# A hybrid decoder layer on one core: the recurrence's rounds joined in pairs, the first gate sums moved to another engine

## The chip, the cores and the metric

The kernel runs on one core of a Trainium2 chip. Five engines work side by side, each with its own queue of instructions: TensorE (PE in the profile; its weight loads are PEld), VectorE (DVE), ScalarE (ACT), GpSimd (POOL) and SyncE (SP, which here only issues DMAs). They wait for each other by semaphores. Matmul results go to PSUM, which is allotted here in banks of 128 partitions by 512 four-byte columns; everything else lies in SBUF. The metric is the device time of one execution in microseconds; the times below are the median of 3 runs.

## The reference, cut to what matters

One layer on x of 1024 tokens by 1024 channels (batch 1): a joint projection, three branches (an RWKV-7 recurrence with 8 heads of 64, a stick-breaking attention, a cross-attention to 256 memory tokens), gates, an output projection, and a convolutional feed-forward part. The change touches the first norm, the recurrence and the feed-forward part:

```python
h = rms_norm(x, norm1_g);  proj = h @ w_in
# recurrence, one token t, per head; S is 64x64
sa = einsum('bhij,bhj->bhi', S, -kk_t)
S  = S * w_t + sa[..., None] * (kk_t * a_t) + v_t[..., None] * k_t
y_t = einsum('bhij,bhj->bhi', S, r_t)
...
h   = rms_norm(x, norm2_g) @ w_up               # 1024 -> 2 * 2816
acc = conv_b + causal_conv_width_3(h, conv_w)
gate, val = split(acc, 2);  x = x + (silu(gate) * val) @ w_down
```

## The kernel before

All large products are float32 products made of three: every operand is split into a high part, which ACT copies (L81, L1502), and a low part, the rest, which POOL or the DVE subtracts (L82, L1505); high by high, high by low and low by high are added in PSUM. Every matmul is issued by one helper (L123), every transposing one by another (L106), so the profile tells matmuls apart by their tiles: `mm` and `g` are the PSUM banks of the large products (128x512) and of the rest.

**Startup.** The projection of the first columns runs over eight blocks of x (`units`, `part_units`), while ACT squares the blocks and the DVE adds the squares (L221). `row_norm` sums the squares over the channels with 32 tiny matmuls and turns them into a factor per token, `row_spread` spreads it. `row_norm` stands inside the fifth block of the second group of columns.

**The recurrence (`stage2`).** The 1024 tokens are 16 chunks of 64, two to a group of 128; the 8 heads are 4 pairs `p`. Within a chunk the recurrence is rewritten as products of 64x64 matrices with the running state `U`. Each pair has a PSUM bank of its own in a chunk (tag `g`, four of them), with 64 columns each for A, Y, W and S. A chunk has three rounds:

1. state products into A and products with `M` onto it, and the DVE copies A into `ys` (L638);
2. products into W, which ACT copies (L649);
3. state products into Y; then, pair by pair, products onto Y, products into S, the DVE's update of the state from S (L659), and ACT's two copies of Y into the output (L661).

Between two rounds `weave` runs steps of the other work (the gates' and the output projection's large products, called filler here), 2.15 steps a round on average, in practice 12 or 18 large matmuls. Every third round or so a part of the output's norm (L680 to L694) is given out, too. The DVE and ACT take their work in the order in which a scheduler put it; among it are evacuations of the filler's banks (L1263).

**The feed-forward part (`up_phase`).** The two-by-two product of weights and tokens is done in seven products instead of eight, on sums of blocks. A loop runs over pairs `n` of weight tiles; `step(n, i)` issues product `i` and what follows from it on the DVE; `prep1`, `prep2`, `prep3` and `second_sums` make the sums and the parts of later weights, mostly on POOL (L1505 low parts, L1520 and L1521, L1540 and L1541 sums). For n=2 the order is 5, 6, 2, 7, 4, 3. Each finished pair of tiles is convolved (`conv`: ACT L1574, DVE L1575, L1584) and becomes a gated tile in `g_all` (L1580, L1587, L1592). `act_sums` makes four sums of the gated tile's quarters for the down phase (DVE, L1600) and stores sums and quarters from ACT's queue (L1605, L1609, L1610). For the first tile it is called in step 6 and step 7 of n=2, where L1637 adds step 6's result, and L1646 and L1647 add step 7's; TensorE's step 3 takes the bank that L1647 reads. L1659 and L1668 follow steps 4 and 3.

Of the kernel before, what the change touches and what calls it, by code (L numbers as in the profile page):

```python
# [49 lines left out]
class Trunk:  # L50
# [135 lines left out]
    def startup(self):  # L186
# [104 lines left out]
        nc.sync.dma_start(self.lora, self.I["lora"])  # L291
        self.seg = self.t4("A")
        nc.sync.dma_start(self.seg, self.I["seg"])
        units(1, [4])
        part_units(1, 5, ((0, 0),), None)
        self.row_norm(sqs[-1])
        part_units(1, 5, ((1, 0), (0, 1)), None)
        units(1, [6, 7])
        units(2, [4])
        self.row_spread()  # L300
# [276 lines left out]
    def stage2(self):  # L577
        nc = self.nc
        self.y = [self.t4("qk") for _ in range(4)]
        vs = self.t4("ys", n=512)  # L580
        it = self.t4("it")
        ut = it[:, 0:512].rearrange("p (u c) -> p u c", u=8)
        U = [[ut[:, 2 * p + i] for i in range(2)] for p in range(4)]
        self.ordered(nc.gpsimd.memset(ut, 0.0))
        hq = [slice(0, 64), slice(64, 128)]
        heads = [(p, h2) for p in range(4) for h2 in range(2)]
        A, Y, W, S = (slice(o, o + 64) for o in range(0, 256, 64))
        Ms = self.t4("at")
        Ls, VTs = {}, {}
        norm = iter(())  # L590

        def load_l(g):
            for p in range(3):
                L = self.t4("at")
                nc.sync.dma_start(L, self.scr[p, g])
                Ls[g, p] = L[:, 0:256], L[:, 256:512], L[:, 512:1024]
            M = Ms[:, g % 2 * 512 : g % 2 * 512 + 512]
            nc.sync.dma_start(M, self.scr[3, g][:, 512:1024])
            Ls[g, 3] = [None, None, M]

        def load_v(g):
            for k in range(2):
                V2 = self.t4("qk")
                for h2 in range(2):
                    nc.sync.dma_start(V2[hq[h2], h2 * 256 : h2 * 256 + 256], self.vd[k, h2, g].rearrange("s c i -> s (c i)"))
                nc.sync.dma_start(V2[:, 512:768], self.td[k, g].rearrange("h s p i -> (h s) (p i)"))
                for i in range(2):
                    VTs[g, 2 * k + i] = [V2[:, h2 * 256 + i * 128 : h2 * 256 + i * 128 + 128] for h2 in range(2)], V2[:, 512 + i * 128 : 640 + i * 128]
                nc.sync.dma_start(V2[:, 768:1024], self.scr[3, g][:, k * 256 : k * 256 + 256])
                Ls[g, 3][k] = V2[:, 768:1024]  # L610

        load_l(0)
        yield
        load_v(0)
        for _ in range(2):
            yield
        for c in range(NC):
            g, cc = c // 2, c % 2
            us = []
            for p in range(4):  # L620
                (RA, BT, MT), (V, TT) = Ls[g, p], VTs[g, p]
                us.append((
                    U[p][cc], U[p][1 - cc], RA[:, cc * 128 : (cc + 1) * 128], BT[:, cc * 128 : (cc + 1) * 128],
                    MT[:, cc * 256 : (cc + 1) * 256], [v[:, cc * 64 : (cc + 1) * 64] for v in V],
                    TT[:, cc * 64 : (cc + 1) * 64], vs[:, p * 64 : (p + 1) * 64], self.ps("g")))

            def state(o, rs):
                for p, h2 in heads if c else ():
                    Uo, _, ra, _, _, _, _, _, pb = us[p]
                    q = hq[h2]  # L630
                    self.mmul(pb[q, o], ra[q, rs], Uo[q], start=True, stop=False)

            state(A, Y)
            for p, h2 in heads:
                _, _, _, _, M, wv, _, v1, pb = us[p]
                self.mmul(pb[hq[h2], A], M[hq[h2], h2 * 128 + 64 : h2 * 128 + 128], wv[h2][hq[h2]], start=(c == 0), stop=True)
                if h2 == 1:
                    nc.vector.tensor_copy(v1, pb[:, A])  # L638
            yield
            next(norm, None)  # L640
            if not cc and g + 1 < NG:
                load_l(g + 1)
                load_v(g + 1)
            for p, h2 in heads:
                _, _, _, _, _, wv, tt, v1, pb = us[p]
                self.mmul(pb[hq[1 - h2], W], tt[hq[h2]], v1[hq[h2]], start=True, stop=True)
                if h2 == 1:
                    for q, w in zip(hq, wv[::-1]):
                        nc.scalar.activation(w[q], pb[q, W], AF.Copy)  # L649
            yield  # L650
            next(norm, None)
            state(Y, A)
            for p, (Uo, Un, ra, bt, M, wv, tt, v1, pb) in enumerate(us):
                for h2, q in enumerate(hq):
                    self.mmul(pb[q, Y], M[:, h2 * 128 : h2 * 128 + 64], wv[h2], start=(c == 0), stop=True)
                if c < NC - 1:
                    for h2, q in enumerate(hq):
                        self.mmul(pb[q, S], bt[:, q], wv[h2], start=True, stop=True)
                    nc.vector.scalar_tensor_tensor(Un, Uo, self.pc[p][:, c : c + 1], pb[:, S], ALU.mult, ALU.add)  # L659
                for h2, q in enumerate(hq):  # L660
                    nc.scalar.activation(self.y[p][cc * 64 : cc * 64 + 64, g * 128 + h2 * 64 : g * 128 + h2 * 64 + 64], pb[q, Y], AF.Copy)  # L661
            yield
            next(norm, None)
            if c % 4 == 3:
                for _ in norm:
                    pass
                norm = self.norm_quarter(c // 4, it[:, 512:1024])
        for _ in norm:
            pass
        for _ in range(4):  # L670
            yield
# [803 lines left out]
    def up_phase(self, raws, t2, operand, split_hi, split_lo, sums, norm, spread):  # L1475
# [21 lines left out]
                    if n < 3:  # L1497
                        self.pinned(ins)

        def hl(src, pool, tags, n=1024, keep=False, queue=False, eng=nc.gpsimd):  # L1500
            hi, lo = (pool.tile([128, n], F32R, name=self.nm(t), tag=t, bufs=16 if t == "l4" else 2) for t in tags)
            ins = nc.scalar.activation(hi, src, AF.Copy)  # L1502
            if keep:
                self.pinned(ins)
            ins = eng.tensor_tensor(lo, src, hi.bitcast(F32), ALU.subtract)  # L1505
            if queue:
                self.tc.keep_in_program_order(ins)
            return hi, lo

        L, R = slice(0, 512), slice(512, 1024)  # L1510
# [21 lines left out]
        def prep3(n):  # L1532
            if n == 0:
                w2, s4 = self.early[2], self.early[3][:, R]
            else:
                w1, w2 = W.pop(n)
                s = st.pop((n, "s"))
                s4 = self.pool_r.tile([128, 512], F32, name=self.nm("s4"), tag="s4", bufs=1)
                fix = self.tc.keep_in_program_order if n == 1 else lambda ins: ins
                fix(nc.gpsimd.tensor_tensor(w2[:, L], w1[:, L], w2[:, L], ALU.subtract))  # L1540
                fix(nc.gpsimd.tensor_tensor(s4, w1[:, R], s[:, R], ALU.subtract))  # L1541
            w = hl(w2, self.pool_wt, ("wh", "wl"), keep=n < 2, queue=n < 2, eng=nc.gpsimd if n else nc.vector)
            st[n, 7], st[n, 4] = [[x[:, c] for x in w] for c in (L, R)]
            if n == 1:
                return s4
            if n:
                st[n, 3] = hl(s4, self.pool_l, ("l4", "l4"), 512)
# [50 lines left out]
        def act_sums(f, late):  # L1598
            a11, a21, a12, a22 = (g_all[:, j] for j in range(4))
            tt = lambda o, x, y, op: self.pinned(nc.vector.tensor_tensor(o, x, y, op))  # L1600
            if not late:
                tt(sa[:, 0], a21, a22, ALU.add)
                tt(sa[:, 1], sa[:, 0], a11, ALU.subtract)
                for j, src in ((0, a11), (1, a12), (3, a22)):
                    nc.scalar.dma_start(self.actd[f, j], src)  # L1605
            else:
                tt(sa[:, 2], a11, a21, ALU.subtract)
                tt(sa[:, 3], a12, sa[:, 1], ALU.subtract)
                nc.scalar.dma_start(self.actd[f, 2], sa[:, 3])  # L1609
                nc.scalar.dma_start(self.actd[f, 4:7].rearrange("i p t -> p i t"), sa[:, 0:3])  # L1610

        def evacuate(n):
            p1 = st[n, "p1"] = self.r4("p1", n=512)
# [4 lines left out]
        def step(n, i):  # L1618
# [13 lines left out]
            elif i == 6:  # L1632
# [4 lines left out]
                self.pinned(nc.vector.tensor_tensor(st[n, "u1"][:, R2], Bk, st[n, "p1"], ALU.add))  # L1637
                if n == 2:
                    st.pop((1, "gates"))[1]()
                if n and pairs[n - 1][2]:  # L1640
                    act_sums(pairs[n - 1][1], n > 2)
            elif i == 7:
                Bk = st.pop((n, "B"))
                product(n, 7, Bk, False, True)
# [2 lines left out]
                ins = nc.vector.tensor_tensor(v[:, R2], st[n, "C"], v[:, L2], ALU.add)  # L1647
                if n == 2:
                    self.pinned(ins)
                    act_sums(pairs[n - 1][1], True)  # L1650
            elif i == 40:
                Dk = st[n, "D"] = bank()
                product(n, 4, Dk, True, True)
# [93 lines left out]
        for n in range(1, len(pairs)):  # L1747
# [3 lines left out]
            for i in order:  # L1751
# [17 lines left out]
                if n > 1 and i == 2:  # L1769
                    prep1(nxt)  # L1770
                    if n == 2:
                        second_sums(4)
                if i == 3:
                    prep3(nxt)

# [173 lines left out]
    def run(self):  # L1949
# [74 lines left out]
        st2 = self.stage2()  # L2024
        next(st2)
        need("y1")
        self.weave(st2, pump, 2.15, 0)
        self.weave(self.group_norm(), pump, 1, 0)
        drain(pump)
        self.close_gates()  # L2030
# [81 lines left out]
```

## Time and profile before

| | |
|---|---|
| median of 3 runs | 1774.13 us (1772.08 to 1774.95) |
| the profiled execution | 1774.39 us, its span 1772.6 us |
| TensorE busy | 1762.3 us, 99% |
| weight loads (beside it) | 1442.4 us, 81% |
| DVE, ACT, POOL busy | 1180.0, 864.8, 677.3 us |
| mean granted TensorE clock | 0.999 |

In the rows of a profile, `x16` is the number of instructions in the row. A row of a timeline begins with its start and its length in us, then engine, line, operation, tiles written and read, and sizes; square brackets hold the engine's idle time before it and what ended that. A row of the list of waits says which engine and line waited for which, the us in total, how often, and the longest.

### The profile page before, as it was taken

What the parts mean: (1) busy time and instruction counts of PE and PEld (TensorE: products, weight loads), DVE (VectorE), ACT (ScalarE), POOL (GpSimd) and SP (SyncE); (2) the same over time, 40 slices, a digit from 0 to 9 for tenths busy, and PEclk for the clock granted to TensorE, in tenths of its full rate; (3) what the DMA queues carried; (4) which work ended last, traced back from release to release, by engine and by line L of the source; (5) the groups of instructions that cost most, each with busy time, mean ns of one, the idle gap of its engine ahead of it and who ended that gap; (6) DMA issues with size and microseconds to landing.
All of it is one profiled execution on the core that took longest, in us unless ns stands there. A gap on an engine that the chain in (4) does not pass through costs nothing.

```text
span 1772.6 us, 27353 instructions
## 1 busy us (share of the span) xinstructions
PE 1762.3 (99%) x10495; PEld 1442.4 (81%) x10495; DVE 1180.0 (67%) x1666; ACT 864.8 (49%) x1569; POOL 677.3 (38%) x401
## 2 busy tenths in 40 slices
PE   9999999999999999999999999999999999999999
PEld 7777778888888888877778888878888888888887
DVE  5667765788887536434344962687767777795597
ACT  6444344466676635535444434635444445454343
POOL 3221021110120042223333543387677677544454
PEclk9999999999999999999999999999999999999999
DMA  5155674112112343677645643233223233396475
GB/s 212 60 166 179 202 245 136 44 50 68 43 56 90 120 111 101 239 240 271 216 165 179 227 165 119 92 107 111 90 89 114 107 113 110 121 330 212 143 243 209
DMA packets 122772, 261.29 MB, mean 147 GB/s; under 512 B 28681, under 2 KB 43657, under 8 KB 122514
## 3 DMA queue, kind: packets, MB, share of 16 engines
q1 hardware_dynamic: 85026, 193.83, 33.1%
q10 hardware_dynamic: 33840, 53.10, 8.1%
q0 software_dynamic: 3776, 12.62, 2.4%
q8 instruction: 82, 1.34, 0.3%
q14 instruction: 48, 0.39, 0.1%
HBM read 178.99 MB, written 80.48 MB: 146 GB/s over the span
## 4 chain that ended last, share of the span: by engine, by line
PE 48%; issue 1%; POOL 1%; DVE 1%; ACT 0%; DMA 0%; DVEq 0%; POOLq 0%; SPq 0%
PE mm L123 41%; PE g L123 7%; PE g L106 1%; DMA wr<-in_w_up_dram 0%; POOL wl L1505 0%; POOL it L1520 0%; DVE raw L1395 0%; POOL l L1505 0%; POOL s L1541 0%; DVE BT L1413 0%; ACT A L1386 0%; POOL rw L1540 0%; ACT qk L649 0%; ACT BT L1408 0%; POOL it L1521 0%
## 5 line engine op out<-in xcount | busy, mean ns | idle before, releaser
L123 PE MATMUL mm<-xhi,wh 128*128 128x512 f32 x784 | 258.0, 410 | 0.1
L123 PE MATMUL mm<-xlo,wh 128*128 128x512 f32 x784 | 243.5, 391 | 0.2 <-DVE xlo L212 0.2
L123 PE MATMUL mm<-xhi,wl 128*128 128x512 f32 x784 | 242.3, 390 | 0.2 <-POOL wl L82 0.2
L82 POOL TENSOR_TENSOR wl<-wr,wh 128x1024 fp32r<-128x1024 f32 (+2 forms) x37 | 89.9, 2430 | 276.3 <-ACT wh L81 267.5
L123 PEld LDWEIGHTS mm<-xlo,wh 128*128 128x128 f32 x784 | 147.2, 188 | 33.5 <-DVE xlo L212 0.7
L123 PEld LDWEIGHTS mm<-xhi,wl 128*128 128x128 f32 x784 | 146.9, 188 | 32.9 <-POOL wl L82 0.8
L123 PEld LDWEIGHTS mm<-xhi,wh 128*128 128x128 f32 x784 | 136.8, 189 | 26.5 <-issue 5.1
L81 ACT ACTIVATE wh<-wr 128x1024 fp32r<-128x1024 f32 (+2 forms) x78 | 81.8, 1049 | 134.7 <-PE mm L123 114.6
L123 PE MATMUL mm<-dw,da 128*128 128x512 f32 x528 | 120.3, 389 | 0.0
L123 PE MATMUL mm<-BT,l 128*128 128x512 f32 x504 | 117.6, 389 | 0.0
L123 PEld LDWEIGHTS mm<-dw,da 128*128 128x128 f32 x528 | 99.1, 188 | 20.6
L1818 POOL TENSOR_TENSOR dw<-draw,dw 128x512 fp32r<-128x512 f32 x55 | 81.8, 1496 | 76.5 <-ACT dw L1816 72.6
L123 PEld LDWEIGHTS mm<-BT,l 128*128 128x128 f32 x504 | 94.6, 188 | 19.6
L123 PE MATMUL mm<-BT,wh 128*128 128x512 f32 x352 | 108.6, 390 | 0.1
L123 PE MATMUL mm<-B,wh 128*128 128x512 f32 x352 | 108.5, 389 | 0.0
L948 DVE TENSOR_TENSOR_SCAN at<-at,nrt 128x128 f32<-128x128 f32 (+3 forms) x64 | 86.2, 1352 | 30.9 <-ACT at L942 30.4
L1817 DVE TENSOR_TENSOR da<-draw,da 128x512 fp32r<-128x512 f32 x77 | 64.9, 848 | 51.3 <-ACT da L1815 49.4
L788 POOL TENSOR_TENSOR hn<-hn,eps 128x16 f32<-128x16 f32 (+1 forms) x12 | 8.5, 707 | 223.1 <-ACT hn L787 223.1
L123 PE MATMUL g<-dw,da 128*128 128x512 f32 x396 | 90.2, 389 | 0.0
L1815 ACT ACTIVATE da<-draw 128x512 fp32r<-128x512 f32 x77 | 48.1, 628 | 79.5 <-PE mm L123 32.0
L123 PEld LDWEIGHTS g<-dw,da 128*128 128x128 f32 x396 | 74.3, 188 | 15.4
L1574 ACT ACTIVATE g<-u,params 128x512 f32<-128x512 f32 x88 | 65.1, 770 | 40.3 <-DVE u L1668 26.7
(350 smaller groups left out, 4008.8 us busy)
## 6 DMA issues: line engine op xcount, KB each, us to landing
wr<-in_w_in_dram SPq DMA_DIRECT2D x48, 512.0 KB, 3.7
draw<-actd SPq DMA_DIRECT2D x77, 256.0 KB, 3.6
draw<-in_w_down_dram SPq DMA_DIRECT2D x55, 256.0 KB, 4.4
at<-scr SPq DMA_DIRECT2D x24, 512.0 KB, 6.3
wr<-in_w_up_dram SPq DMA_DIRECT2D x22, 512.0 KB, 3.4
actd<-gall ACTq DMA_DIRECT2D x44, 256.0 KB, 3.1
rw<-in_w_up_dram SPq DMA_DIRECT2D x20, 512.0 KB, 3.8
gsd<-w ACTq DMA_DIRECT2D x18, 512.0 KB, 3.1
```

The costliest lines, as they stand in the source:

```text
L81: (fix_hi or fix)(self.nc.scalar.activation(hi, raw, AF.Copy))
L82: fix(self.low.tensor_tensor(lo, raw, hi.bitcast(F32), ALU.subtract))
L106: self.pinned(self.nc.tensor.transpose(out, in_, self.ident[:n, :n]))
L123: self.pinned(self.nc.tensor.matmul(*a, **k))
L788: nc.gpsimd.tensor_tensor(v3(t), v3(t), self.eps.unsqueeze(2).to_broadcast([128, 8, nh]), ALU.add)
L948: self.pinned(nc.vector.tensor_tensor_scan(sn[:, :W][:, ::-1], sn[:, :W][:, ::-1], self.nrt[:, 1152 - W :][:, ::-1], 1.0, ALU.mult, ALU.max))
L1574: nc.scalar.activation(c, u[:, 2 + h * 512 : 514 + h * 512], AF.Identity, scale=self.par("cw2", m), bias=self.par("cb", m))
L1815: self.pinned(nc.scalar.activation(A[:, 0], a, AF.Copy))
L1817: self.pinned(nc.vector.tensor_tensor(A[:, 1], a, A[:, 0].bitcast(F32), ALU.subtract))
L1818: nc.gpsimd.tensor_tensor(Wt[:, 1], w, Wt[:, 0].bitcast(F32), ALU.subtract)
```

## The change

Four edits, each in its own place:

- **Recurrence.** The four banks are now allotted once per group. The second chunk of a group uses columns 256 to 511 of the banks in which the first used 0 to 255. In a group's first chunk the third round begins with the products into S and the state's update, ahead of the state products into Y; and there is no filler after it: the second chunk's products with `M` into A follow at once, and the state products are added to them. Filler is 2.55 steps a round in place of 2.15.
- **Gate sums.** Of the first tile's four sums one stays on the DVE (in step 6 of n=2), three go to POOL, behind `second_sums(4)`. The stores of three quarters stay in ACT's queue, those of the sums go to SP's.
- **Low part.** For n=1 the low part that `prep3` makes is subtracted in two halves of 512 columns, the right half first.
- **Startup.** `row_norm` stands behind the whole fifth block, not inside it.

```diff
-        units(1, [4])
-        part_units(1, 5, ((0, 0),), None)
+        units(1, [4, 5])
         self.row_norm(sqs[-1])
-        part_units(1, 5, ((1, 0), (0, 1)), None)
...
         for c in range(NC):
             g, cc = c // 2, c % 2
+            if not cc:
+                banks = [self.ps("g") for _ in range(4)]
+            A, Y, W, S = (slice(o, o + 64) for o in range(256 * cc, 256 * cc + 256, 64))
...
-            def state(o, rs):
+            def state(o, rs, begin=True):
                 for p, h2 in heads if c else ():
-                    Uo, _, ra, _, _, _, _, _, pb = us[p]
+                    Uo, _, ra, _, _, _, _, v1, pb = us[p]
                     q = hq[h2]
-                    self.mmul(pb[q, o], ra[q, rs], Uo[q], start=True, stop=False)
+                    self.mmul(pb[q, o], ra[q, rs], Uo[q], start=begin, stop=not begin)
+                    if not begin and h2 == 1:
+                        nc.vector.tensor_copy(v1, pb[:, o])
...
-                self.mmul(pb[hq[h2], A], M[hq[h2], h2 * 128 + 64 : h2 * 128 + 128], wv[h2][hq[h2]], start=(c == 0), stop=True)
-                if h2 == 1:
+                self.mmul(pb[hq[h2], A], M[hq[h2], h2 * 128 + 64 : h2 * 128 + 128], wv[h2][hq[h2]], start=(c == 0 or cc == 1), stop=not cc)
+                if h2 == 1 and not cc:
                     nc.vector.tensor_copy(v1, pb[:, A])
+            if cc:
+                state(A, last, False)
+                next(norm, None)
             yield
...
+            def states(p):
+                Uo, Un, ra, bt, M, wv, tt, v1, pb = us[p]
+                for h2, q in enumerate(hq):
+                    self.mmul(pb[q, S], bt[:, q], wv[h2], start=True, stop=True)
+                nc.vector.scalar_tensor_tensor(Un, Uo, self.pc[p][:, c : c + 1], pb[:, S], ALU.mult, ALU.add)
+
+            if not cc:
+                for p in range(4):
+                    states(p)
+            state(Y, first)
...
+            if not cc:
+                continue
             yield
...
-            ins = eng.tensor_tensor(lo, src, hi.bitcast(F32), ALU.subtract)
+            for c in cuts or (slice(0, n),):
+                ins = eng.tensor_tensor(lo[:, c], src[:, c], hi[:, c].bitcast(F32), ALU.subtract)
...
+        def first_sums():
+            for o, x, y in ((1, sa[:, 0], g_all[:, 0]), (2, g_all[:, 0], g_all[:, 1]), (3, g_all[:, 2], sa[:, 1])):
+                self.tc.keep_in_program_order(nc.gpsimd.tensor_tensor(sa[:, o], x, y, ALU.subtract))
+            nc.sync.dma_start(self.actd[0, 2], sa[:, 3])
+            nc.sync.dma_start(self.actd[0, 4:7].rearrange("i p t -> p i t"), sa[:, 0:3])
...
-                if n and pairs[n - 1][2]:
-                    act_sums(pairs[n - 1][1], n > 2)
+                    self.pinned(nc.vector.tensor_tensor(sa[:, 0], g_all[:, 1], g_all[:, 3], ALU.add))
+                    sent(0)
+                elif n and pairs[n - 1][2]:
+                    act_sums(pairs[n - 1][1], True)
...
                 if n == 2:
                     self.pinned(ins)
-                    act_sums(pairs[n - 1][1], True)
...
                     if n == 2:
                         second_sums(4)
+                        first_sums()
...
-        self.weave(st2, pump, 2.15, 0)
+        self.weave(st2, pump, 2.55, 0)
```

What moves on the engines. TensorE, before, between the last round of a group's first chunk and the first round of its second (`g_7649` to `g_7652` are the first chunk's banks, `g_7789` on the second's; `mm` is filler, of which only the ends are shown; in brackets the engines whose work an instruction waits for):

```order
L123 MATMUL g_7651<-qk_7259,at_7251 64x64 x4
L123 MATMUL g_7652<-qk_7259,at_6795 64x64 x2
L123 MATMUL g_7652<-qk_7259 64x64 x2
L123 MATMUL mm_7587<-xhi_288,wh_7471 128x512
...
L123 MATMUL mm_7777<-yhi_7568,wl_7580 128x512 [waits Pool_49]
L123 MATMUL mm_7778<-yhi_7568,wl_7580 128x512
L123 MATMUL g_7789<-it_6793,at_7535 64x64 [waits DMAHW7_49,DVE_49,Activation_49]
L123 MATMUL g_7789<-it_6793,at_7535 64x64
L123 MATMUL g_7790<-it_6793,at_7537 64x64 [waits DMAHW0_49,DVE_49,Activation_49]
```

The same place in a joined round after (`g_7481` to `g_7484` are the banks of both chunks; `it` is the state, so the first two rows are the last pair's state products into Y, the next four the products onto Y, and the rest the second chunk's products into A):

```order
L123 MATMUL g_7484<-it_6793,qk_7259 64x64 [waits DVE_49]
L123 MATMUL g_7484<-it_6793,qk_7259 64x64
L123 MATMUL g_7481<-qk_7259,at_7252 64x64 x2
L123 MATMUL g_7482<-qk_7259,at_7254 64x64 x2
L123 MATMUL g_7483<-qk_7264,at_7256 64x64 x2
L123 MATMUL g_7484<-qk_7264,at_6795 64x64 x2
L123 MATMUL g_7481<-qk_7259,at_7252 64x64 [waits Activation_49]
L123 MATMUL g_7481<-qk_7259,at_7252 64x64
L123 MATMUL g_7482<-qk_7259,at_7254 64x64 [waits Activation_49]
L123 MATMUL g_7482<-qk_7259,at_7254 64x64
```

The filler between the chunks is gone, and the waits for the DVE and for ACT stand among the small products.

POOL before, from the part of weights for n=3 on (`it` is what `second_sums(4)` makes):

```order
L1505 TENSOR_TENSOR wl_11046<-wr_10885,wh_11045 128x1024
L1520 TENSOR_TENSOR it_11049<-rw_10999 128x512
L1521 TENSOR_TENSOR it_11049<-it_11049,rw_10998 128x512
L1540 TENSOR_TENSOR rw_10999<-rw_10998,rw_10999 128x512
L1505 TENSOR_TENSOR wl_11129<-wr_10886,wh_11128 128x1024
```

And after (lines are numbered anew: L1522 is the old L1505, L1537 and L1538 the old L1520 and L1521, L1557 the old L1540):

```order
L1522 TENSOR_TENSOR wl_11014<-wr_10854,wh_11013 128x1024
L1537 TENSOR_TENSOR it_11017<-rw_10968 128x512
L1538 TENSOR_TENSOR it_11017<-it_11017,rw_10967 128x512
L1634 TENSOR_TENSOR gall<-gall 128x512 x3
L1557 TENSOR_TENSOR rw_10968<-rw_10967,rw_10968 128x512
L1522 TENSOR_TENSOR wl_11098<-wr_10855,wh_11097 128x1024
```

Three sums stand behind the old L1521. On the DVE, before:

```order
L1580 TENSOR_TENSOR gall<-g_10971,gall 128x512
L1600 TENSOR_TENSOR gall<-gall 128x512 x2
L1566 MEMSET u_11064 128x2
L1646 TENSOR_TENSOR u_11064<-mm_11002,p_1653_10951 128x512
L1647 TENSOR_TENSOR u_11064<-mm_10985,u_11064 128x512
L1600 TENSOR_TENSOR gall<-gall 128x512 x2
L1659 TENSOR_TENSOR u_11064<-u_11064,mm_11072 128x512
```

and after (L1597 is the old L1580, L1674, L1675 and L1686 the old L1646, L1647 and L1659):

```order
L1597 TENSOR_TENSOR gall<-g_10940,gall 128x512
L1666 TENSOR_TENSOR gall<-gall 128x512
L1583 MEMSET u_11037 128x2
L1674 TENSOR_TENSOR u_11037<-mm_10971,p_1621_10920 128x512
L1675 TENSOR_TENSOR u_11037<-mm_10954,u_11037 128x512
L1686 TENSOR_TENSOR u_11037<-u_11037,mm_11041 128x512
```

One sum is left ahead of the two additions, none behind them. In the recurrence's joined rounds the old L638 and L659 are L633 or L642 and L663, the old L661 is L675.

More of the change, by code (lines that the diff above doesn't have):

```diff
@@ L586, in stage2 @@
         heads = [(p, h2) for p in range(4) for h2 in range(2)]
-        A, Y, W, S = (slice(o, o + 64) for o in range(0, 256, 64))
         Ms = self.t4("at")
@@ L624, in stage2 @@
                     MT[:, cc * 256 : (cc + 1) * 256], [v[:, cc * 64 : (cc + 1) * 64] for v in V],
-                    TT[:, cc * 64 : (cc + 1) * 64], vs[:, p * 64 : (p + 1) * 64], self.ps("g")))
-            def state(o, rs):
+                    TT[:, cc * 64 : (cc + 1) * 64], vs[:, p * 64 : (p + 1) * 64], banks[p]))
+            def state(o, rs, begin=True):
                 for p, h2 in heads if c else ():
-                    Uo, _, ra, _, _, _, _, _, pb = us[p]
+                    Uo, _, ra, _, _, _, _, v1, pb = us[p]
                     q = hq[h2]
-                    self.mmul(pb[q, o], ra[q, rs], Uo[q], start=True, stop=False)
-            state(A, Y)
+                    self.mmul(pb[q, o], ra[q, rs], Uo[q], start=begin, stop=not begin)
+                    if not begin and h2 == 1:
+                        nc.vector.tensor_copy(v1, pb[:, o])
+            first, last = slice(0, 64), slice(64, 128)
+            if not cc:
+                state(A, last)
             for p, h2 in heads:
                 _, _, _, _, M, wv, _, v1, pb = us[p]
-                self.mmul(pb[hq[h2], A], M[hq[h2], h2 * 128 + 64 : h2 * 128 + 128], wv[h2][hq[h2]], start=(c == 0), stop=True)
-                if h2 == 1:
+                self.mmul(pb[hq[h2], A], M[hq[h2], h2 * 128 + 64 : h2 * 128 + 128], wv[h2][hq[h2]], start=(c == 0 or cc == 1), stop=not cc)
+                if h2 == 1 and not cc:
                     nc.vector.tensor_copy(v1, pb[:, A])
+            if cc:
+                state(A, last, False)
+                next(norm, None)
             yield
@@ L651, in stage2 @@
             next(norm, None)
-            state(Y, A)
+            def states(p):
[7 more added lines that the diff above has]
+            state(Y, first)
             for p, (Uo, Un, ra, bt, M, wv, tt, v1, pb) in enumerate(us):
@@ L655, in stage2 @@
                     self.mmul(pb[q, Y], M[:, h2 * 128 : h2 * 128 + 64], wv[h2], start=(c == 0), stop=True)
[L656 to L659, printed above, removed]
+                if cc and c < NC - 1:
+                    states(p)
                 for h2, q in enumerate(hq):
                     nc.scalar.activation(self.y[p][cc * 64 : cc * 64 + 64, g * 128 + h2 * 64 : g * 128 + h2 * 64 + 64], pb[q, Y], AF.Copy)
+            if not cc:
+                continue
             yield
@@ L1498, in load, with hl @@
                         self.pinned(ins)
-        def hl(src, pool, tags, n=1024, keep=False, queue=False, eng=nc.gpsimd):
+        def hl(src, pool, tags, n=1024, keep=False, queue=False, eng=nc.gpsimd, cuts=None):
             hi, lo = (pool.tile([128, n], F32R, name=self.nm(t), tag=t, bufs=16 if t == "l4" else 2) for t in tags)
@@ L1504, in hl @@
                 self.pinned(ins)
-            ins = eng.tensor_tensor(lo, src, hi.bitcast(F32), ALU.subtract)
-            if queue:
-                self.tc.keep_in_program_order(ins)
+            for c in cuts or (slice(0, n),):
+                ins = eng.tensor_tensor(lo[:, c], src[:, c], hi[:, c].bitcast(F32), ALU.subtract)
+                if queue:
+                    self.tc.keep_in_program_order(ins)
             return hi, lo
@@ L1541, in prep3 @@
                 fix(nc.gpsimd.tensor_tensor(s4, w1[:, R], s[:, R], ALU.subtract))
-            w = hl(w2, self.pool_wt, ("wh", "wl"), keep=n < 2, queue=n < 2, eng=nc.gpsimd if n else nc.vector)
+            w = hl(w2, self.pool_wt, ("wh", "wl"), keep=n < 2, queue=n < 2, eng=nc.gpsimd if n else nc.vector, cuts=(R, L) if n == 1 else (slice(0, 1024),))
             st[n, 7], st[n, 4] = [[x[:, c] for x in w] for c in (L, R)]
@@ L1603, in act_sums @@
                 tt(sa[:, 1], sa[:, 0], a11, ALU.subtract)
-                for j, src in ((0, a11), (1, a12), (3, a22)):
-                    nc.scalar.dma_start(self.actd[f, j], src)
+                sent(f)
             else:
@@ L1610, in act_sums, with sent @@
                 nc.scalar.dma_start(self.actd[f, 4:7].rearrange("i p t -> p i t"), sa[:, 0:3])
+        def sent(f):
+            for j, src in ((0, 0), (1, 2), (3, 3)):
+                nc.scalar.dma_start(self.actd[f, j], g_all[:, src])
+        def first_sums():
[3 more added lines that the diff above has]
+            nc.sync.dma_start(self.actd[0, 4:7].rearrange("i p t -> p i t"), sa[:, 0:3])
         def evacuate(n):
```

## The prediction

> **What bounds the kernel now.** I read the page first, then who waits on TensorE, then the chain that ended last, and last the timelines of single stretches. The page's first lines:
>
> ```profile
> span 1772.6 us, 27353 instructions
> PE 1762.3 (99%) x10495; PEld 1442.4 (81%) x10495; DVE 1180.0 (67%) x1666; ACT 864.8 (49%) x1569; POOL 677.3 (38%) x401
> ```
>
> TensorE is busy 1762.3 of 1772.6 us; its stalls, each with what ended it, are few (waited for, total us, times, longest):
>
> ```profile
> PE mm L123 <- DVE u L1647: 2.8, 1, 2.8
> ...
> PE g L123 <- DVE ys L638: 0.6, 1, 0.6
> PE mm L123 <- POOL wl L1505: 0.5, 1, 0.5
> PE g L123 <- DVE qk L221: 0.4, 1, 0.4
> ```
>
> The four parts of the change stand beside these four rows. None removes a matmul, so all that can be won lies in such stalls and at the seams between big and small matmuls; and whatever makes TensorE wait anew counts in full, as the end of the chain (start, length, engine, line, instructions) leaves no idle time to give it back in:
>
> ```profile
> 850.59 2.95 PE mm L123 x12
> 853.54 1.69 PE g L123 x48
> ...
> 1208.08 381.39 PE mm L123 x1680
> 1589.47 29.92 PE g L123 x132
> ```
>
> In the recurrence (the first two rows of this fence are a filler and a last round) small rounds and fillers follow each other without a gap. A round of 48 records is 24 products of 64x64, two records each: 0.070 us a product. 132 large matmuls in 29.92 us are 0.227 each, so a filler of 12 is 2.72 of work in 2.95: a seam pair costs 0.23.
>
> **Recurrence: what goes.** Sixteen chunks of three rounds were 48 rounds; joined they are 40. Filler steps stay about the same (48 x 2.15 = 103, 40 x 2.55 = 102), so 8 seam pairs go: 8 x 0.23 = -1.8 us. The one wait for L638 (0.6) is a chance of order and may come back anywhere; I put it at 0.
>
> **Recurrence: what comes.** Before, what a round leaves to the DVE (state update L659) and to ACT (output copies L661) runs under the next filler. Start, length, engine, line:
>
> ```profile
> 854.63 0.75 DVE L659 SCALAR_TENSOR_TENSOR it<-it,pc,g 128x64 f32<-128x64 f32 x3 [2.10 <-issue]
> 854.95 1.86 ACT L661 ACTIVATE qk<-g 64x64 f32<-64x64 f32 x8 [2.84 <-DVE it L659]
> 858.13 0.56 PE L123 MATMUL g<-it,at 64*64 64x64 f32 x12
> ```
>
> The copies end at 856.81 and the next round starts at 858.13: hidden, 1.3 us to spare. In the joined round that filler is gone, and the order shows the waits inside the 40 products: the state products for Y of each pair wait for the DVE (that pair's state update read the same bank), and the second chunk's first products of each pair wait for ACT (that pair's two output copies). The columns are others, the bank is the same. That this program does wait by bank the old trace shows too: ACT's output copy, which reads the columns Y, sat idle until the DVE had read the columns S:
>
> ```profile
> L661 ACT ACTIVATE qk<-g x128: 216/219/223, 765.3 to 961.0; 64x64 f32<-64x64 f32 x128
> its engine sat idle before it (us, times) until:
>   DVE it L659: 32.9, 15
> ```
>
> [...]
>
> The joined round's length, from its first state product at 0. Lags first:
>
> ```profile
> 849.59 0.61 DVE L638 COPY ys<-g 128x64 f32<-128x64 f32 x4
> 849.86 0.72 PE L123 MATMUL g<-ys,qk 64*64 64x64 f32 x16 [0.56 <-DVE ys L638]
> 850.24 1.87 ACT L649 ACTIVATE qk<-g 64x64 f32<-64x64 f32 x8 [4.27 <-PE g L123]
> L638 DVE COPY ys<-g x64: 206/214/226, 757.9 to 951.4; 128x64 f32<-128x64 f32 x64
> L659 DVE SCALAR_TENSOR_TENSOR it<-it,pc,g x60: 269/279/283, 765.0 to 945.8; 128x64 f32<-128x64 f32 x60
> ```
>
> The first copy ends at 849.59 + 0.21 = 849.80 and TensorE starts at 849.86: 0.06. ACT starts 0.24 after two products (850.00); the update at 854.63 starts 0.25 after the twelfth product of its round (853.54 + 0.84). Three updates take 0.75 and one 0.28: a pitch of 0.235. Eight ACT copies take 1.86 and one 0.22: a pitch of 0.234.
> - State products of four pairs: 0 to 0.56. Updates: first 0.14 + 0.25 = 0.39, fourth 1.10 to 1.38.
> - Products of the state for Y: the last pair's at 1.38 + 0.06 = 1.44 to 1.58; then the Y products to 2.14.
> - The first Y pair is done at 1.72; copies 1.96 to 3.82.
> - The second chunk's last pair starts at 3.82 + 0.06 = 3.88, ends 4.02; eight more state products: 4.58.
> Forty products alone are 2.80, so 1.78 us of stall a round; eight rounds, +14.2.
>
> On the DVE's queue two 512-wide operations, in most groups L1263 evacuations of the filler, stand right ahead of the first update of every joined round:
>
> ```profile
> 848.05 1.29 DVE L1263 TENSOR_TENSOR w<-mm,w 128x512 f32<-128x512 f32 x2 [5.36 <-DMA w<-gsd]
> ```
>
> If their matmul is long past they cost nothing. If it is the filler's last, the update starts at 0.25 + 1.29 = 1.54 in place of 0.39, and the round is 1.1 longer. Between 0 and 1.1 I take the middle, 0.5, eight times: +4.0 (0 to +9). Recurrence: 14.2 + 4.0 - 1.8 = +16.4, bounds +12 and +21 if the waits bite, -1.8 if they don't.
>
> **Startup.** The column sums wait for the last square sum:
>
> ```profile
> 31.25 1.10 PE L123 MATMUL g<-kon,qk 128*64 128x1 f32 x32 [0.40 <-DVE qk L221]
> ```
>
> Four matmuls go ahead of it, 4 x 0.227 = 0.9 us, more than the wait: -0.4. The cover between the norm and its spread falls from 22 matmuls to 18 (5.0 to 4.1 us); before, nothing waited behind those 22, and how much was to spare isn't shown. If none, the 0.4 comes back: -0.4 to +0.5; I take -0.4.
>
> **Gate sums.** Before (n=2):
>
> ```profile
> 1184.60 0.69 DVE L1580 TENSOR_TENSOR gall<-g,gall 128x512 f32<-128x512 f32 x1
> 1185.32 5.71 DVE L1600 TENSOR_TENSOR gall<-gall 128x512 f32<-128x512 f32 x2
> 1190.96 0.68 DVE L1646 TENSOR_TENSOR u<-mm,p 128x512 f32<-128x512 f32 x1
> 1191.68 0.69 DVE L1647 TENSOR_TENSOR u<-mm,u 128x512 f32<-128x512 f32 x1
> ```
> ```profile
> 1185.32 2.38 POOL L1505 TENSOR_TENSOR l<-it,l 128x1024 fp32r<-128x1024 f32 x1
> 1187.66 2.82 POOL L1505 TENSOR_TENSOR wl<-wr,wh 128x1024 fp32r<-128x1024 f32 x1
> 1190.44 1.72 POOL L1520 TENSOR_TENSOR it<-rw 128x512 f32<-128x512 f32 x1
> ```
> ```profile
> 1192.51 4.58 PE L123 MATMUL mm<-B,l 128*128 128x512 f32 x12 [2.78 <-DVE u L1647]
> 1192.85:1196.27 3.42, 3.42 (x10) 2.68 (x9) 3.42 (x3) 0.00 (x0) 2.35 (x2) 0.50 0.54 214
> ```
>
> Two sums of 0.69 elsewhere took 5.71 while POOL ran its subtractions, and TensorE's step 3 waited for L1647 behind them. The last row is a window's busy time by engine and then the granted clock: 0.50 for 3.42 us right after the 2.78 of idling, so some 1.7 us more were lost. With one sum left there (about half of 5.71, 2.86, as POOL still runs beside it) L1647 ends at 1185.32 + 2.86 + 1.4 = 1189.6, and step 3 starts at about 1189.8 in place of 1192.5: -2.7, and -1.7 with the clock kept: -4.4.
>
> What it may wake: POOL gets three more operations of 1.3 (the width of L1520, which takes that where the DVE is quiet), ahead of its next weights, and is busy to about 1196.5, which is no later than the 1200.34 at which the next low part of weights started before. The DVE's next gate product overwrites the third input of the last sum and so waits for it to 1196.5, with L1668 and the convolutions behind it; L1637 of n=3, at 1207.34 before, then comes at some 1203 for a TensorE that arrives 4.5 us earlier than here:
>
> ```profile
> 1207.34 0.69 DVE L1637 TENSOR_TENSOR u<-mm,p 128x512 f32<-128x512 f32 x1
> 1208.08 0.73 PE L123 MATMUL mm<-BT,wh 128*128 128x512 f32 x2
> 1200.34 2.41 POOL L1505 TENSOR_TENSOR wl<-wr,wh 128x1024 fp32r<-128x1024 f32 x1 [5.14 <-ACT wh L1502]
> ```
>
> That is level within half a microsecond: -2.5 to -4.7, taken as -4.4. The four stores leave ACT's queue or go earlier; the two moved to SP's wait for POOL's sums ahead of a weight load that waits for that low part of POOL's anyway: 0.
>
> **Low part in halves (n=1).**
>
> ```profile
> 1162.61 2.40 POOL L1505 TENSOR_TENSOR wl<-wr,wh 128x1024 fp32r<-128x1024 f32 x1 [3.14 <-ACT wh L1502]
> 1165.06 0.50 PE L123 MATMUL mm<-BT,wl 128*128 128x512 f32 x1 [0.53 <-POOL wl L1505]
> 1167.97 2.39 POOL L1505 TENSOR_TENSOR wl<-rw,wh 128x1024 fp32r<-128x1024 f32 x1
> 1170.68 0.39 PE L123 MATMUL mm<-B,wl 128*128 128x512 f32 x1
> ```
>
> The half that is used first is ready at 1163.9, so the 0.5 goes. But the next low part is ready at 1170.36 as before, 0.3 ahead of its use at 1170.68: the 0.5 meets a wait there, and POOL runs without a gap from there to the gate sums. 0, at best -0.5.
>
> **Sum.** +16.4 - 0.4 - 4.4 + 0 = +11.6 us. The profiled execution took 1774.39 (span 1772.6), 0.26 above the median of 1774.13; on the median the forecast is 1785.7.
>
> **The rivals.**
> 1. *The joined rounds don't stall; faster.* If the copies and updates ran fully under products, the -1.8, -0.4 and -4.4 would stay: 1767.5. It decides at a stall of 0.83 us a round (6.6 / 8). For it: TensorE loads weights ahead, and no old trace has a joined round. Against: eight copies at 0.234 can't be shorter than 1.86, and only Y products and first products lie beside them.
> 2. *About even.* Only the copies bite: if the updates were done in time, the Y products would follow at 1.12 in place of 1.58, and 0.46 of the 1.78 would go. 8 x 1.32 = 10.6, less 6.6: 1778.1, and within 0.2% with a copy pitch a tenth shorter. For it: the bounds of the update's lag rest on one round each; against: the evacuations only add.
> 3. *The clock falls in the joined rounds too.* Before, 2.78 us idle halved it for 3.42, a loss of 1.7. A joined round has 1.8 to 2.9 us of idle in pieces of under 1.5. If it falls in every one: 8 x 1.7 = 13.6, 1799. Against: the 0.56 of L638 left the clock at 1.00. [...]
> 4. *POOL's sums hold the DVE up* (L1637 of n=3 late by up to 2): up to 1787.7, inside the forecast's own range.
>
> **Chances.** Forecast 0.64, its own range 1780 (recurrence +12, the rest as summed, rounded) to 1791 (recurrence +21); rival 1 0.15, rival 2 0.13, rival 3 0.08. 0.2% is 3.5 us, about what a measurement of this kernel tells from no change. Faster: rival 1 and the edge of 2, 0.17; same: most of what is left of rival 2, 0.10; slower: the rest, 0.73. The range takes in rivals 1 and 2 and leaves out the clock's: 1767 to 1792.
>
> **What would show it.** Right: TensorE's waits list gains the new L663 (update) and L675 (output copy) with some 8 and 24 to 32 entries and 14 to 20 us; the wait for the old L1647 shrinks under 0.5 and the clock stays 1.00 from 1190 on (shifted); the L221 row goes. Wrong: joined rounds of 40 products that last under 3.6 us; a clock of 0.5 between 760 and 980; a new wait of TensorE on POOL or on L1663 at n=3.

## The result, and the profile after

The change makes the kernel slower: 1787.75 us against 1773.92 (medians of 6 runs each), +13.8; the ratio is 1.0086 (95% interval 1.0075 to 1.0097). The forecast was 1785.7, slower, within 1767 to 1792. The profile is of an execution of 1790.43 us, 2.7 above the median; what is peculiar to it is said below.

The page after, and whom TensorE's matmuls waited for (us in all, times, longest):

```profile
span 1788.6 us, 27364 instructions
PE 1770.9 (99%) x10495; PEld 1448.3 (81%) x10495; DVE 1180.4 (66%) x1663; ACT 864.6 (48%) x1569; POOL 679.9 (38%) x405
```
```profile
PE g L123 <- DVE it L663: 4.0, 3, 3.0
PE mm L123 <- DVE u L1663: 2.4, 1, 2.4
PE g L123 <- ACT qk L675: 1.2, 6, 0.2
...
PE mm L123 <- POOL wl L1522: 0.4, 1, 0.4
```

The old rows of L1647 and L221 are gone, and the two new ones of the recurrence are there, for the update (L663) and the output copies (L675). But they name 5.2 us only. A matmul row that is held up by a semaphore ahead of each pair counts as one long busy row (1.75 us for sixteen records that take 0.69 without a wait, below); what it waited for stands in the list of the weight loads (PEld), which name 14.3 us in 39 entries:

```profile
PEld g L123 <- ACT qk L675: 8.4, 30, 0.3
PEld g L123 <- DVE it L663: 5.9, 9, 3.1
```

The timeline of the joined round at 791.29 shows the long row, and one of the weight loads inside it (start, length):

```profile
791.29 0.57 PE L123 MATMUL g<-qk,at 128*64 128x64 f32 x12
791.69 0.29 PE L123 MATMUL g<-qk 128*64 128x64 f32 x4
792.07 0.71 PE L123 MATMUL g<-it,at 64*64 64x64 f32 x12
792.64 0.33 PE L123 MATMUL g<-it,qk 64*64 64x64 f32 x4
792.90 0.69 PE L123 MATMUL g<-qk,at 128*64 128x64 f32 x16
793.79 1.75 PE L123 MATMUL g<-qk,at 64*64 64x64 f32 x16 [0.20 <-ACT qk L675]
795.38 0.52 PE L123 MATMUL g<-it,at 64*64 64x64 f32 x12
795.73 0.28 PE L123 MATMUL g<-it,qk 64*64 64x64 f32 x4
795.94 0.73 PE L123 MATMUL mm<-yhi,wh 128*128 128x512 f32 x2
```
```profile
794.26 0.20 PEld L123 LDWEIGHTS g<-qk,at 64*64 64x64 f32 x4 [0.28 <-ACT qk L675]
```
```profile
791.73 0.85 DVE L663 SCALAR_TENSOR_TENSOR it<-it,pc,g 128x64 f32<-128x64 f32 x4 [2.83 <-issue]
793.28 1.87 ACT L675 ACTIVATE qk<-g 64x64 f32<-64x64 f32 x8 [3.30 <-PE g L123]
```

The rows at 792.90 and 793.79, of 16 records each, hold eight products; without a wait that is 0.69, as at 792.90. At 793.79 the second chunk's eight products took 1.75, because they run at the pace of the eight copies of 793.28. The round is 795.94 - 791.29 = 4.65 us; worked out were 4.58, with the updates at 0.39 (0.44 here) and the copies at 1.96 (1.99 here).

From start to start of what follows, the eight joined rounds are 3.87 (the first, without products of `U` into Y), 4.65, 8.46, 4.64, 5.36, 5.35, 4.66 and 4.90: 20.1 us over the products alone. The longest one, at 817.41, is a case of its own (DVE, then POOL, then TensorE):

```profile
817.15 3.70 DVE L1250 TENSOR_TENSOR A<-A,yhi 128x1024 fp32r<-128x1024 f32 x2 [2.13 <-ACT yhi L1249]
820.77 0.84 DVE L663 SCALAR_TENSOR_TENSOR it<-it,pc,g 128x64 f32<-128x64 f32 x4
```
```profile
816.25 2.38 POOL L82 TENSOR_TENSOR wl<-wr,wh 128x1024 fp32r<-128x1024 f32 x1
```
```profile
821.10 0.91 PE L123 MATMUL g<-it,at 64*64 64x64 f32 x12 [3.00 <-DVE it L663]
```
```profile
817.41:825.87 8.46, 5.46 (x82) 4.44 (x81) 4.66 (x9) 2.99 (x10) 1.79 (x2) 0.65 0.98 353
825.87:832.20 6.33, 6.33 (x20) 4.78 (x19) 0.41 (x2) 0.00 (x0) 0.00 (x0) 0.66 0.33 107
```

Two low parts of 1024 stand ahead of the update on the DVE; they took 3.70, the first of them 2.56 beside POOL's subtraction (one takes 1.2 elsewhere). TensorE stood for 3.00, and meanwhile the clock fell (to 0.50 from 819.95 on): the last two rows are windows (busy time by engine, granted clock, DMA share, GB/s) of that round and of the filler behind it, with a mean clock of 0.65 and 0.66. From the end of the wait the round took 4.77, where the round at 791.29 took 3.87 from the same product on, and the filler of 18 took 6.33 in place of some 4.3.

In the feed-forward part the stall of 2.78 is gone. Its place, DVE and TensorE, and the one thing that it woke:

```profile
1202.56 2.92 DVE L1666 TENSOR_TENSOR gall<-gall 128x512 f32<-128x512 f32 x1
1206.13 0.69 DVE L1675 TENSOR_TENSOR u<-mm,u 128x512 f32<-128x512 f32 x1
1214.15 0.69 DVE L1604 TENSOR_TENSOR gall<-g,sg 128x512 f32<-128x512 f32 x1 [2.73 <-POOL gall L1634]
1219.96 0.69 DVE L1663 TENSOR_TENSOR u<-mm,p 128x512 f32<-128x512 f32 x1
```
```profile
1206.96 2.99 PE L123 MATMUL mm<-B,l 128*128 128x512 f32 x12
1220.70 0.73 PE L123 MATMUL mm<-BT,wh 128*128 128x512 f32 x2
```

Step 3's twelve products took 2.99 with the clock kept (1.00), in place of 4.58. The DVE did wait 2.73 for POOL's last sum, and L1663 (the old L1637) ends at 1220.65, 0.05 ahead of TensorE's need at 1220.70: level, as worked out, and no more.

The 2.4 us on L1663 in the list of waits lie elsewhere, at 1356, and belong to this execution: two stores on ACT's queue took 3.15 us to issue (the same pair took 0.93 in the profile before), which delayed a convolution and moved two gate sums of the DVE into POOL's next subtraction (the two took 3.47). No profile of the experiments below shows it.

```profile
1345.70 3.15 ACTq L1630 DMA_DIRECT2D actd<-gall  x2
1356.62 0.74 PE L123 MATMUL mm<-BT,wh 128*128 128x512 f32 x2 [2.35 <-DVE u L1663]
```

### The profile page after: what moved, and what is told of

Read it like the earlier page. It is cut to its first block, busy times and chain, and to the rows that moved or that the text cites. A ratio compares the mean times of both kernels' runs of the same rounds, so it can differ in the third digit from the quotient of the medians.

```text
span 1788.6 us, 27364 instructions
## 1 busy us (share of the span) xinstructions
PE 1770.9 (99%) x10495; PEld 1448.3 (81%) x10495; DVE 1180.4 (66%) x1663; ACT 864.6 (48%) x1569; POOL 679.9 (38%) x405
## 4 chain that ended last, share of the span: by engine, by line
PE 45%; DVE 2%; POOL 2%; issue 2%; DMA 1%; ACT 1%; SPq 0%; ACTq 0%; DVEq 0%; POOLq 0%
PE mm L123 39%; PE g L123 5%; POOL dw L1846 1%; PE g L106 1%; DMA at<-scr 0%; ACT qk L675 0%; DVE g L1592 0%; POOL it L1537 0%; POOL wl L1522 0%; DVE g L1601 0%; DMA draw<-in_w_down_dram 0%; DVE gall L1609 0%; DMA wr<-in_w_up_dram 0%; DVE da L1845 0%; POOL l L1522 0%
```

## The experiments

Times are medians; the kernel before, run beside them, had 1773.6 to 1774.0.

**1. The recurrence alone.** The diff of `stage2` and the 2.55, on the kernel before.

> The kernel before with the recurrence's edit alone. Theory (the joined rounds stall TensorE by their own waits): 8 joined rounds of 4.6 to 5.4 us in place of 2.8, one of them 8.5 as in the profile after, and 2 us of halved clock behind it: 20 + 2 - 2 for the seams, about +17 us or a little more, 1790 to 1793. Rival (the recurrence costs less alone, the other edits delay its inputs): under +12.

Measured: 1790.72, ratio 1.0095 (1.0081 to 1.0109), +17.1. The joined rounds have the lengths of the profile after to 0.02 us (8.44 for the long one), and the old waits of 2.8 for L1647 and 0.4 for L221 are back. The recurrence is the whole loss; its rival falls.

**2. Everything but the recurrence.** `stage2` and the 2.15 as before.

> The changed kernel with the recurrence of before; gate sums, halved low part and startup as changed. Theory: -4.4 for the gate sums and -0.4 for the startup, 1769 (1768 to 1770.5). Rival (what the gate sums win is given back further on, as the DVE waits 2.7 us for POOL there): 1772 to 1774.

Measured: 1768.86, ratio 0.9973 (0.9963 to 0.9982), -4.8. It is faster than both kernels. The DVE's wait for POOL stands there too, with 2.46; TensorE's small waits near it are both ahead of those sums, and none follows:

```profile
1196.05 0.69 DVE L1586 TENSOR_TENSOR gall<-g,sg 128x512 f32<-128x512 f32 x1 [2.46 <-POOL gall L1616]
```
```profile
1169.54 0.50 PE L123 MATMUL mm<-B,wl 128*128 128x512 f32 x1 [0.43 <-POOL wl L1504]
1183.36 0.73 PE L123 MATMUL mm<-BT,wh 128*128 128x512 f32 x2 [0.37 <-DVE u L1645]
```

**3. The filler back, the new order kept.**

```diff
                 state(A, last, False)
-                next(norm, None)
             yield
...
-            if not cc:
-                continue
             yield
...
-        self.weave(st2, pump, 2.55, 0)
+        self.weave(st2, pump, 2.15, 0)
```

> The changed kernel with the filler put back between a group's two chunks (48 rounds of 2.15 steps), while the shared banks and the state products ahead of the outputs stay. Theory (the missing filler uncovers the output copies; the order adds a smaller wait for the state's update): the copies are hidden again, the wait for the update stays with 0.5 to 1.0 a group, 4 to 8 us over the kernel with the old recurrence: 1773 to 1777. Rival (sharing a bank between chunks is the cost by itself): 1784 or more.

Measured: 1778.13, ratio 1.0029 (1.0020 to 1.0039). No wait for the output copies is left; those for the update stay, and cost more than I put down:

```profile
PE g L123 <- DVE it L662: 4.3, 5, 2.1
PE g L195 <- DVE offs L167: 1.2, 1, 1.2
```

A round with the state products ahead is 2.2 to 2.9 us where its 24 products took 1.69 before, one is 5.26, and the filler of 18 behind that one took 5.46: its first rows of two matmuls, from 925.99 to 928.62, took 1.22, 1.05 and 0.91, the later ones 0.61 to 0.63.

**4. Joined, but in the old order.**

```diff
-            if not cc:
-                for p in range(4):
-                    states(p)
             state(Y, first)
...
-                if cc and c < NC - 1:
+                if c < NC - 1:
                     states(p)
```

> The changed kernel with joined rounds, but in each group's first chunk the outputs' state products first again and the products into S after the Y products. Theory: no wait of TensorE for the update, the copies start 0.5 us earlier, a joined round is 4.1 us in place of 4.65: -4 us, 1784. Rival (the order ahead is what keeps the stall small, since the update must be done before the second chunk's state products): +2 to +5, 1790 to 1793.

Measured: 1781.07, ratio 1.0043 (1.0029 to 1.0057): 6.7 us under the changed kernel. Five of the joined rounds are 4.11 to 4.14 where 4.1 was worked out. The first is 3.57, the one at 900.09 is 4.70, and the one behind the two low parts 6.84, 1.6 less than in the changed kernel; with the filler behind it, 1.3 shorter, that is most of the gain over the 4 us expected. TensorE no longer waits for the update at all:

```profile
PE g L123 <- ACT qk L672: 3.3, 8, 1.7
PE g L195 <- DVE offs L167: 1.2, 1, 1.2
```

**5. Half of the copies on the DVE.**

```diff
-                    nc.scalar.activation(self.y[p][...], pb[q, Y], AF.Copy)
+                    yo = self.y[p][...]
+                    if cc or not h2:
+                        nc.scalar.activation(yo, pb[q, Y], AF.Copy)
+                    else:
+                        nc.vector.tensor_copy(yo, pb[q, Y])
```

> The changed kernel, but in each group's first chunk the second of a pair's two output copies is made by the DVE, not by ACT. Theory (eight ACT copies in a row, 0.234 each, pace the joined round): four of them take half the time, the last pair's products start 0.7 to 0.9 us earlier, a joined round is 3.8 in place of 4.65: -6 us, 1782 (1780 to 1783.5). Rival (the products wait for the state's update and the lags between engines, not for the pace of the copies): within 1 us of the changed kernel, 1787 to 1789.

Measured: 1778.45, ratio 1.0026 (1.0016 to 1.0036): 9.3 us under the changed kernel. All eight rounds became shorter, by 0.83 to 1.22 (3.67 for 4.65), 8.0 in all; the filler behind the long one is 1.3 shorter. ACT's copies stand in a row of 0.57 in place of 1.87:

```profile
793.52 0.76 PE L123 MATMUL g<-qk,at 64*64 64x64 f32 x16 [0.23 <-DVE qk L679]
```
```profile
792.99 0.57 ACT L677 ACTIVATE qk<-g 64x64 f32<-64x64 f32 x4 [3.31 <-PE g L123]
```

The same eight products, 0.76 in place of 1.75. So the pace of ACT's copies set about half of a usual round's stall (0.98 of the 1.85 over its products); the rival falls. My bounds were 1.5 us short of the gain: a round came out at 3.67, not 3.8, and they had nothing for the clock.

**6. The low parts off the DVE.**

```diff
-            self.pinned(self.nc.vector.tensor_tensor(los[k], y, hi[:, k].bitcast(F32), ALU.subtract))
+            self.pinned(self.nc.gpsimd.tensor_tensor(los[k], y, hi[:, k].bitcast(F32), ALU.subtract))
```

> The changed kernel with the low parts of the branches' outputs (L1250, eight in all) subtracted on POOL, not on the DVE. Theory (the 8.5 us round and the halved clock behind it come from two of these standing ahead of the state's update in the DVE's queue): that round is 4.7 to 5.4, TensorE's wait of 3.0 for the update and the halved clock are gone, -4 to -6 us: 1782 to 1784. Rival (something else makes that round late, or POOL is late with them and the filler waits): 1786 or more.

Measured: 1784.31, ratio 1.0059 (1.0046 to 1.0071), 3.4 under the changed kernel, 0.3 outside my bounds. The long round is 5.47 and keeps its clock, as the theory has it. But the clock now fell in another round, at 900.55, and its filler took 6.53:

```profile
817.93:823.40 5.47, 4.02 (x82) 3.05 (x81) 1.11 (x6) 4.11 (x12) 5.44 (x4) 1.00 0.98 344
900.55:906.45 5.90, 5.11 (x82) 3.87 (x81) 2.48 (x9) 3.65 (x13) 3.85 (x2) 0.82 0.21 85
906.45:912.98 6.53, 6.53 (x21) 4.92 (x19) 1.75 (x5) 0.00 (x0) 1.38 (x2) 0.64 0.40 151
```

**7. The gate sums alone.** The diff of `act_sums`, `sent`, `first_sums` and `step`, on the kernel before.

> The kernel before with the gate sums' edit alone. Theory: the 2.8 us stall and the halved clock behind it go: -4.4, 1769.5. Rival (given back behind): -1 to -2.

Measured: 1769.46, ratio 0.9974 (0.9963 to 0.9984): -4.5. The list of waits has no row for L1647's place, and the clock is 1.00 there:

```profile
1190.00:1198.00 8.00, 8.00 (x37) 6.60 (x36) 4.30 (x8) 4.92 (x9) 7.92 (x8) 1.00 0.43 153
```

**8. Shared banks alone.** Experiments 3 and 4 together: filler and order as before, the banks and the second chunk's order within A as changed.

> The changed kernel with the filler between the chunks (48 rounds of 2.15) and with the old order of products inside a chunk: of the recurrence's edit the shared banks and the second chunk's products ahead of its state products stay. Theory (sharing banks costs only where nothing stands between the chunks): as with the old recurrence, 1769 (1768 to 1771). Rival (the bank itself costs, filler or not): 1773 or more.

Measured: 1769.08, ratio 0.9973 (0.9963 to 0.9983), 0.2 from experiment 2; between 753 and 975 us TensorE waits for nothing. Sharing a bank cost nothing here while a filler stood between its reader and its next writer. From experiment 3 to this one only the order differs: state products ahead cost 9.1 us there.

**9. Startup and halved low part alone.**

> The kernel before with the startup's edit and the halved low part alone. Theory (the startup wins its wait of 0.4, and the low part's 0.5 is met again at the next low part): -0.4, 1773.5, and within 0.2% of before; the wait list loses L221 and shows one wait of 0.4 to 0.5 for a low part, at another product. Rival (the halves are worth their 0.5 as well, and the clock or the gate sums' stall gains with them): -1 to -2.

Measured: 1773.59, ratio 0.9999 (0.9990 to 1.0008): no difference. L221 is off the list, and the wait for a low part has moved to the next one, with nearly its size:

```profile
1169.66 0.50 PE L123 MATMUL mm<-B,wl 128*128 128x512 f32 x1 [0.44 <-POOL wl L1504]
```

## Why the prediction was right

- *The bound.* TensorE had no slack, and what made it wait counted in full: the parts measured alone, +17.1, -4.5 and -0.1, make +12.5 of the +13.8, within what medians with intervals of 0.2 to 0.3% can tell.
- *Recurrence, +16.4.* Measured +17.1 alone and +18.9 as the last part added (1787.75 - 1768.86). The undisturbed joined round, 4.58 worked out, was 4.65. The two waits in it were shown apart: taking the wait for the update away brought 4.65 to 4.12 (experiment 4), halving the copies brought it to 3.67 (5), and a filler between the chunks took the copies' wait away (3, 8). The parts do not quite add up: 20.1 in the rounds and 2.0 in the filler behind the long one, less 1.8 for the seams, are 20.3 where 18.9 came. No run measured the seams alone, and 1.4 us stay open.
- *The evacuations ahead of the update*, 4.0 between 0 and 9, were the weakest term. That it came out near, 20.1 - 8 x 1.8 = 5.7, was luck, as it was not mostly by that mechanism. Five of the eight rounds lost 0 to 0.3 there. One lost 0.7 to evacuations, which ran until 879.44 in the round of 878.20, and one 0.7 at 905.03, where ACT's copies of W were late too. The long one lost 3.8: 2.9 to two low parts that my 1.29 for evacuations didn't cover, the rest to the lower clock within the round. The 2.56 of the first of them beside POOL's subtraction, in place of 1.2, is what L1600 had shown in the feed-forward part before (5.71 for two sums of 0.69), and I did not carry it over.
- *The clock.* I gave the halved clock 0.08, as a matter of all eight rounds or none. It fell at one round each in the profiles of the changed kernel and of experiments 1 and 4, at the longest stall (a mean of 0.65, 0.69 and 0.87 in the round), and in experiment 6 elsewhere (0.82); in experiments 3 and 5 the rows behind the longest stall show it (1.22 us for the filler's first two matmuls, 0.73 in other fillers). It cost 0.7 to 2.2 us in the filler behind, and 0.9 more in the long round of the changed kernel. As a rival for the whole it was wrong, as a term it was missing.
- *What would show it.* I expected some 8 and 24 to 32 entries and 14 to 20 us in the rows of L663 and L675. The list of the matmuls held 9 entries and 5.2 us, that of the weight loads 9 and 30 entries and 14.3 us: the sign was there, in the weight loads' rows. One sign of being wrong came as well, a clock of 0.5 between 760 and 980; it belongs to the term that was missing.
- *Gate sums, -4.4.* Measured -4.5: step 3 without stall and with full clock. Rival 4, the DVE's wait for POOL, happened with 2.73 and did not reach TensorE.
- *Low part, 0, and startup, -0.4.* Together -0.1, in an interval of 0.1% either way; the halves' 0.5 was met by the next low part (0.44), as forecast.
- *Rival 1* fell: no joined round of the changed kernel was under 3.87. *Rival 2* had the copies' share right, not the updates': in experiment 4, where only the copies' wait is left, most rounds lose the 1.32 worked out for it, and the long round (2.7 over the others) and the clock bring its 1778.1 to 1781.07. In the changed kernel the updates' wait is there, too.

For waits by the shared bank the runs show this much: the second chunk's products, which write other columns of the same banks, went at the pace of the copies (1.75 us for eight, 0.76 with half of the copies on the DVE). Joined rounds with a bank of their own for each chunk were not run, nor a kernel without the waits: that the shared bank alone makes them is argued from the order of the instructions, and that the chip needs them is not shown.

## What to carry to other kernels

Filler between two dependent rounds pays for its seams (0.23 us a pair here) by hiding the slower engine's turn: by estimate (8 x 0.23), eight copies of 0.23 us on ACT need 1.9 us of other work on TensorE before the next write to their banks. Before joining rounds, count what each reader of a bank still has to do when the next writer arrives, and give the readers to two engines if it must be done. Test the edits of one change apart: here one was worth -4.5 us and lay buried under another's +17.

## What the runs showed of the hardware that I had not expected

The granted clock fell in a stretch without one long stall. In experiment 6 the round at 900.55 has listed waits of its matmuls of 0.21 and 0.20 us, its clock fell on the way (mean 0.82) and its filler ran at a mean of 0.64, while the profile after has a round of the same work at 905.03, 5.35 us long, and no such fall in the filler behind it. What decides which of them is hit no run shows; what lay ahead the windows show. Leaving out the kernel's start and end, the clock fell once in the profile before and once in the profile after, to 0.50 both times: for 3.42 us from 1192.85 on, and for 10.24 from 819.95 on. In the 3.41 us ahead TensorE was busy for 0.63 in the one and for 1.55 in the other; ahead of the fall in experiment 6 it was busy for 2.71, as much as in the round that kept its clock. The first two windows below are of the profile after, the third is of experiment 6, ahead of its fall, and the last of the profile after, where none followed (in the last two, rows that wait count as busy):

```profile
816.54:819.95 3.41, 1.55 (x21) 0.98 (x19) 2.80 (x2) 2.07 (x4) 2.66 (x2) 1.00 1.03 420
819.95:830.19 10.24, 9.10 (x74) 7.34 (x75) 2.53 (x9) 1.76 (x8) 0.00 (x0) 0.50 0.76 253
```
```profile
900.96:904.37 3.41, 2.71 (x50) 2.05 (x48) 1.59 (x6) 2.55 (x9) 1.77 (x1) 1.00 0.18 74
```
```profile
905.29:908.70 3.41, 2.71 (x52) 1.96 (x46) 1.74 (x6) 2.54 (x9) 1.63 (x1) 1.00 0.25 102
```

The list of the matmuls' waits alone can be far too small: 5.2 us where the rounds lost some 20. A row of small products that wait for one semaphore a pair is shown as one busy row, so the checks are the row's length against the same row without waits (1.75 against 0.69) and the list of the weight loads (14.3 us).
